# Folded column tiles: the accumulator's last big reader takes its scalar from PSUM, and the two extra columns are copied behind it

## The chip, the core and the metric

One NeuronCore of a Trainium2 chip runs the whole program. The metric is the device time of one execution in microseconds (us). TensorE (PE in the profile) multiplies, VectorE (DVE), ScalarE (ACT) and GpSimd (POOL) work on the results, SyncE (SP) issues loads. Matmul results land in PSUM, everything else lives in SBUF.

## What is computed

One inference step of a two-layer decoder with 256 prompt tokens and 32 sample tokens (8 sequences of 4), 288 token columns in all, model width 1024, in fp32. Per layer:

```python
proj = x @ w_in                       # q, k, v of 12 heads, and a gated unit
att  = dilated_window_attention(q, k, v)   # three head groups; sample tokens also see a cache
x = layer_norm(ALPHA * x + concat(att, sgu) @ w_mix_out, ln1_g, ln1_b)
qx = x @ w_xq;  x = layer_norm(ALPHA * x + cross_attention(qx, mem) @ w_xo, ln2_g, ln2_b)
h = square(relu(x @ w_up));  x = layer_norm(ALPHA * x + h @ w_down, ln3_g, ln3_b)
```

## The kernel before

The activations are kept transposed: 128 features on the partitions, 288 tokens along the free dimension. Each fp32 product is made of three matmuls of rounded parts (`L361` to `L363` in `mm3`): high weights by high activations (`wh`, `xH`), high by low (`wh`, `xL`), low by high (`wl`, `xH`). Weights stream in as 128 columns by 1024 rows; ScalarE rounds them to `wh` (`L343`) and VectorE forms the rest `wl` (`L344`). One output tile of 128 columns is 24 matmuls into one accumulator `acc`, of which there are three; so the fourth tile can start only when the first one's accumulator has been read out.

A layer norm would make TensorE wait: the next projection needs normalised activations. So the first tiles of the projection behind a norm are *folded*: they multiply the not yet normalised activations (`fH`, `fL`, already scaled by g), and the normalisation is done on the result. The operands carry two extra columns, minus g and b, so that a folded accumulator has 290 columns: 288 tokens, then the weights' column sums against minus g and b. `fold` turns such an accumulator into a tile `fy`: `L532` copies the two extra columns to a small SBUF tile `fw`, `L533` computes s * fw[0] + acc (s is the mean, one row of 288 on every partition), `L536` multiplies by q, the reciprocal deviation, on GpSimd for the first four folds of a norm and on VectorE after them. fw[1] goes on as the bias of whoever takes `fy`.

There are 32 folds in five stages: 8 tiles of `w_xq` in each layer, 6 of `w_up` in each layer, and 4 of `w_in` in layer 1. While they run, VectorE and GpSimd make the real normalised activations of the later tiles: `L611` or `L632` subtract the mean, `L615` or `L635` scale, `L625` or `L640` form `xL`. `w_in` of layer 1 has four folded tiles (queries 0 to 3) and then 18 tiles on `xH` and `xL`; its evacuation `evac_in` adds the bias (`L778`) and rotates queries and keys (`rope`: `L723`, `L724` on VectorE, `L725`, `L726` on GpSimd). Behind them come `L1041` and `L804` (transposes of `qT` and `kT`), `L984` (scores of the sample tokens, with `zq` from `L1015`) and, on GpSimd and VectorE, the products of cached keys with queries (`L1059`, `L1061`, `L1062`).

The order on each engine is not that of the code: a scheduler of the framework, which goes by a time model of its own, puts the instructions in order before the program is built. So a changed dependency can move other instructions too. On the chip every engine works its list strictly in order.

Of the kernel before, what the change touches and what calls it, by code (L numbers as in the profile page):

```python
# [12 lines left out]
ALU = mybir.AluOpType  # L13
# [7 lines left out]
TOK = SEQ + NS  # L21
# [207 lines left out]
def build(ctx, tc, I, O, worder, corder, recording):  # L229
    nc = tc.nc  # L230
    V, S, G, T = nc.vector, nc.scalar, nc.gpsimd, nc.tensor
# [8 lines left out]
    def etile(name="e", w=TOK):  # L240
        return sb.tile([128, w], F32, name=name, tag="e", bufs=8)
# [4 lines left out]
    def small(w, name="sm"):  # L246
        return sb.tile([128, w], F32, name=name, tag="small", bufs=12)
# [10 lines left out]
    def tr(name="tr"):  # L258
        return pp.tile([128, 512], F32, name=name, tag="tr", bufs=3)
# [197 lines left out]
    for n in range(KT):  # L457
        ps = tr()
# [40 lines left out]
    class LN:  # L499
# [28 lines left out]
        def fold(self, ps):  # L528

            w = small(2, "fw")  # L530
            e = etile("fy")
            V.tensor_copy(w, ps[:, TOK:TOK + 2])  # L532
            V.scalar_tensor_tensor(out=e, in0=self.s, scalar=w[:, 0:1], in1=ps[:, :TOK],  # L533
                                   op0=ALU.mult, op1=ALU.add)
            self.folds += 1
            (G if self.folds <= FOLD_POOL else V).tensor_mul(e, e, self.q)  # L536
            return e, w[:, 1:2]
# [969 lines left out]
```

## Time and profile before

| | us |
|---|---|
| median of 3 runs | 1071.11 |
| lowest, highest | 1068.39, 1072.94 |
| the profiled execution | 1073.84 |
| span of its records | 1072.1 |
| TensorE busy in the span | 1026.8 |
| VectorE busy in the span | 763.2 |

The span goes from the first to the last instruction; the profiled execution's own time is 1.7 us longer. Of all engines TensorE has the least idle time, 45 us.

### The profile page before, as it was taken

The page shows a single profiled execution, that of the slowest core. Times are in us where ns is not written, and L with a number is a line of the kernel's source. Part 1 is how long each engine was busy: PE and PEld are TensorE (multiplying, and loading weights), DVE is VectorE, ACT ScalarE, POOL GpSimd, SP SyncE. Part 2 cuts the span into 40 slices and gives each one's busy share as a digit, 9 for nine tenths or more (in the row PEclk, how much of TensorE's full clock was granted, in tenths as well). Part 3 has the DMA queues.
Part 4 walks back from the last instruction along what each step waited for, and adds up shares of the span by engine and source line. Part 5 has one row for each costly group of instructions (what it writes and reads, how often), then busy time and mean ns, then how long its engine had stood idle before and what let it go on. Part 6 is the DMA issues. An engine that isn't in the chain of part 4 may idle for free. (4 is left out here: it accounts for less than half of the span.)

```text
span 1072.1 us, 20130 instructions
## 1 busy us (share of the span) xinstructions
PE 1026.8 (96%) x8038; PEld 958.7 (89%) x8038; DVE 763.2 (71%) x1406; ACT 531.0 (50%) x1000; POOL 189.2 (18%) x151
## 2 busy tenths in 40 slices
PE   8999999999999999999988999999999999999995
PEld 7989589988799999999977985998888999999994
DVE  6698679855489756565996876897464996565656
ACT  4427546543458535353562364565353685354431
POOL 5592013000023000000448500220000410000000
PEclk8999999999999999999999999999999999999997
DMA  9999844777944555544455898447874465545431
GB/s 290 299 260 316 243 166 154 245 267 255 325 129 143 190 169 181 158 158 161 155 162 165 241 302 235 141 161 237 285 277 157 142 177 165 185 163 191 165 117 44
DMA packets 185533, 213.68 MB, mean 199 GB/s; under 512 B 5760, under 2 KB 175136, under 8 KB 185440
## 3 DMA queue, kind: packets, MB, share of 16 engines
q1 hardware_dynamic: 177216, 205.00, 60.1%
q10 hardware_dynamic: 8224, 7.41, 2.1%
q8 instruction: 63, 1.03, 0.4%
q14 instruction: 30, 0.25, 0.1%
HBM read 203.80 MB, written 8.59 MB: 198 GB/s over the span
## 5 line engine op out<-in xcount | busy, mean ns | idle before, releaser
L343 ACT ACTIVATE wh<-wraw 128x1024 fp32r<-128x1024 f32 (+1 forms) x237 | 249.3, 1054 | 285.6 <-PE acc L362 234.2
L344 DVE TENSOR_TENSOR wl<-wraw,wh 128x1024 fp32r<-128x1024 f32 (+1 forms) x237 | 308.4, 1304 | 100.1 <-ACT wh L343 99.5
L361 PE MATMUL acc<-xH,wh 128*128 128x288 f32 x728 | 219.0, 301 | 3.2 <-DVE fy L533 3.2
L363 PE MATMUL acc<-xH,wl 128*128 128x288 f32 x728 | 217.3, 299 | 2.7 <-DVE wl L344 2.7
L362 PE MATMUL acc<-xL,wh 128*128 128x288 f32 x728 | 218.5, 301 | 1.2 <-DVE xL L640 1.2
L361 PE MATMUL acc<-hH,wh 128*128 128x288 f32 x512 | 151.1, 295 | 0.0
L362 PE MATMUL acc<-hL,wh 128*128 128x288 f32 x512 | 151.1, 295 | 0.0
L363 PE MATMUL acc<-hH,wl 128*128 128x288 f32 x512 | 150.8, 295 | 0.0
L361 PEld LDWEIGHTS acc<-xH,wh 128*128 128x128 f32 x728 | 139.5, 192 | 4.4 <-issue 2.5
L363 PEld LDWEIGHTS acc<-xH,wl 128*128 128x128 f32 x728 | 138.9, 191 | 4.0 <-DVE wl L344 3.6
L362 PEld LDWEIGHTS acc<-xL,wh 128*128 128x128 f32 x728 | 139.1, 191 | 2.3 <-DVE xL L640 1.9
L551 POOL TENSOR_TENSOR s<-s,xres 128x288 f32<-128x288 f32 x15 | 20.2, 1349 | 444.8 <-DVE s L547 444.1
L361 PEld LDWEIGHTS acc<-hH,wh 128*128 128x128 f32 x512 | 96.4, 188 | 0.0
L362 PEld LDWEIGHTS acc<-hL,wh 128*128 128x128 f32 x512 | 96.4, 188 | 0.0
L363 PEld LDWEIGHTS acc<-hH,wl 128*128 128x128 f32 x512 | 96.2, 188 | 0.0
L361 PE MATMUL acc<-fH,wh 128*128 128x290 f32 x256 | 78.3, 306 | 1.8 <-DVE fy L533 1.8
L362 PE MATMUL acc<-fL,wh 128*128 128x290 f32 x256 | 76.9, 301 | 0.2 <-DVE fL L525 0.2
L363 PE MATMUL acc<-fH,wl 128*128 128x290 f32 x256 | 75.8, 299 | 0.5 <-DVE wl L344 0.5
L361 PEld LDWEIGHTS acc<-fH,wh 128*128 128x128 f32 x256 | 48.3, 189 | 2.6 <-PE acc L363 2.2
L362 PEld LDWEIGHTS acc<-fL,wh 128*128 128x128 f32 x256 | 48.5, 190 | 1.2 <-DVE fL L525 0.6
L363 PEld LDWEIGHTS acc<-fH,wl 128*128 128x128 f32 x256 | 48.1, 189 | 1.2 <-DVE wl L344 1.0
L1059 POOL TENSOR_TENSOR cu<-cu,qb 128x1024 f32<-128x1024 f32 x15 | 43.5, 2917 | 13.1 <-DMA qb<-qd 9.6
(326 smaller groups left out, 2182.2 us busy)
## 6 DMA issues: line engine op xcount, KB each, us to landing
cu<-cache_mem_kv SPq DMA_DIRECT2D x64, 512.0 KB, 7.4
wraw<-w_up SPq DMA_DIRECT2D x32, 1024.0 KB, 5.5
wraw<-w_down SPq DMA_DIRECT2D x32, 1024.0 KB, 4.8
wraw<-w_in SPq DMA_DIRECT2D x21, 1024.0 KB, 5.7
cu<-cache_kv_w SPq DMA_DIRECT2D x42, 512.0 KB, 8.5
wraw<-w_xkv SPq DMA_DIRECT2D x16, 1024.0 KB, 6.4
wraw<-w_mix_out SPq DMA_DIRECT2D x8, 1024.0 KB, 10.1
wraw<-w_xq SPq DMA_DIRECT2D x8, 1024.0 KB, 4.9
```

Source lines behind the costliest of these rows:

```text
L343: S.activation(h[:, r], raw[:, r], AF.Copy)
L344: gates[f"split{k}"] = behind(V.tensor_sub(lo[:, r], raw[:, r], h[:, r].bitcast(F32)), "dve")
L361: m = T.matmul(ps, wh[:, k], H[:, k], start=first, stop=False)
L362: T.matmul(ps, wh[:, k], L[:, k], start=False, stop=False)
L363: T.matmul(ps, wl[:, k], H[:, k], start=False, stop=last)
L551: eng.tensor_add(self.s, self.s, xres[:, n])
L1059: G.tensor_mul(cu, cu, qb[g])
```

## The change

`fold` issues its two VectorE operations the other way round, and the first of them reads its per-partition scalar from the accumulator itself, from column 288 in PSUM, where it read the copy in SBUF before. The copy of the two columns then only serves the bias. In the changed kernel the big operation is `L532` (to `L533`) and the copy is `L534`; all other lines keep their numbers.

```diff
             w = small(2, "fw")
             e = etile("fy")
+            V.scalar_tensor_tensor(out=e, in0=self.s, scalar=ps[:, TOK:TOK + 1], in1=ps[:, :TOK],
+                                   op0=ALU.mult, op1=ALU.add)
             V.tensor_copy(w, ps[:, TOK:TOK + 2])
-            V.scalar_tensor_tensor(out=e, in0=self.s, scalar=w[:, 0:1], in1=ps[:, :TOK],
-                                   op0=ALU.mult, op1=ALU.add)
             self.folds += 1
             (G if self.folds <= FOLD_POOL else V).tensor_mul(e, e, self.q)
             return e, w[:, 1:2]
```

The scheduler answers with another order in all five stages. First VectorE in `w_in` of layer 1, from the first scaling of the norm on; the first pair of lines that differ belongs to the second folded tile (rows with - are of before, with + of the change):

```order
 L635 SCALAR_TENSOR_TENSOR xres<-xres,lnp,q 128x288
-L532 COPY fw<-acc 128x2
+L532 SCALAR_TENSOR_TENSOR fy<-s,acc 128x288
+L534 COPY fw<-acc 128x2
 L635 SCALAR_TENSOR_TENSOR xres<-xres,lnp,q 128x288 x7
 L778 TENSOR_SCALAR fy<-fy,fw 128x288
 L344 TENSOR_TENSOR wl<-wraw,wh 128x1024
 L971 COPY kt<-tr 128x512
-L533 SCALAR_TENSOR_TENSOR fy<-s,fw,acc 128x288
-L640 SCALAR_TENSOR_TENSOR xL<-xres,lnp,xH 128x288 x5
-L532 COPY fw<-acc 128x2
+L640 SCALAR_TENSOR_TENSOR xL<-xres,lnp,xH 128x288
```

Before, the copy stood early and the big operation ten instructions later, just ahead of the `xL` tiles; now both stand at the copy's old place.

On TensorE in the same stage, the changed kernel, from the sixth k-step of the first tile that isn't folded (`acc_6354`; the tile after it is `acc_6389`, the third `acc_6430`):

```order
L361 MATMUL acc_6354<-xH_6122,wh_6244 128x288
L361 MATMUL acc_6389<-xH_6122,wh_6278 128x288
L362 MATMUL acc_6389<-xL_6123,wh_6278 128x288
L362 MATMUL acc_6354<-xL_6123,wh_6244 128x288
L363 MATMUL acc_6354<-xH_6122,wl_6245 128x288
L361 MATMUL acc_6354<-xH_6122,wh_6244 128x288
L363 MATMUL acc_6389<-xH_6122,wl_6279 128x288
```

Before, all 24 matmuls of `acc_6354` stood ahead of the first one of `acc_6389`; now the second tile begins between the last k-steps of the first.

On VectorE in `w_up` (the same in both layers), before, from the eight scalings of the norm to the second folded tile's big operation and the `wl` behind it:

```order
L615 SCALAR_TENSOR_TENSOR xres<-xres,lnp,q 128x288 x8
L532 COPY fw<-acc 128x2
L344 TENSOR_TENSOR wl<-wraw,wh 128x1024
L1438 TENSOR_TENSOR r<-r 128x288
L532 COPY fw<-acc 128x2
L533 SCALAR_TENSOR_TENSOR fy<-s,fw,acc 128x288
L344 TENSOR_TENSOR wl<-wraw,wh 128x1024
```

And the same place in the changed kernel:

```order
L615 SCALAR_TENSOR_TENSOR xres<-xres,lnp,q 128x288 x8
L344 TENSOR_TENSOR wl<-wraw,wh 128x1024
L1438 TENSOR_TENSOR r<-r 128x288
L532 SCALAR_TENSOR_TENSOR fy<-s,acc 128x288
L534 COPY fw<-acc 128x2
L344 TENSOR_TENSOR wl<-wraw,wh 128x1024
```

Here the big operation of the second tile stays where it was, behind `L344` and `L1438`; only two copies ahead of it are gone.

## Rows read from the trace of the kernel before

**Rows 1.** Page, part 1: busy us (share of the span) and instructions of each engine.

```profile
PE 1026.8 (96%) x8038; PEld 958.7 (89%) x8038; DVE 763.2 (71%) x1406; ACT 531.0 (50%) x1000; POOL 189.2 (18%) x151
```

**Rows 2.** Waits of PE: who waited, for whom, us in total, times, longest.

```profile
PE acc L361 <- DVE fy L533: 5.0, 4, 2.1
```

**Rows 3.** Stretches: length, busy (x instructions) of PE, PEld, DVE, ACT, POOL; PEclk, DMA.

```profile
164.00:205.00 41.00, 40.84 (x306) 39.63 (x306) 40.54 (x72) 26.77 (x50) 7.80 (x8) 1.00 0.61 202
528.00:562.00 34.00, 28.50 (x194) 26.17 (x192) 33.59 (x66) 20.42 (x40) 14.82 (x15) 0.95 0.51 159
552.00:558.00 6.00, 4.73 (x26) 4.76 (x27) 6.00 (x12) 0.17 (x1) 4.79 (x5) 0.72 0.46 159
562.00:600.00 38.00, 32.97 (x238) 30.17 (x238) 29.87 (x46) 12.40 (x24) 33.72 (x22) 0.91 0.57 180
586.00:594.00 8.00, 7.20 (x30) 5.96 (x31) 8.00 (x10) 0.84 (x2) 8.00 (x6) 0.57 0.65 214
```

**Rows 4.** Timeline of PE: start, us, instruction, [idle before, releaser].

```profile
335.24 0.37 PE L361 MATMUL acc<-fH,wh 128*128 128x290 f32 x1 [0.93 <-DVE fy L533]
...
545.59 0.37 PE L361 MATMUL acc<-xH,wh 128*128 128x288 f32 x1 [1.09 <-DVE fy L533]
...
546.90 0.40 PE L362 MATMUL acc<-xL,wh 128*128 128x288 f32 x1 [0.31 <-DVE xL L640]
...
550.68 0.40 PE L362 MATMUL acc<-xL,wh 128*128 128x288 f32 x1 [0.90 <-DVE xL L640]
...
553.27 0.58 PE L361 MATMUL acc<-xH,wh 128*128 128x288 f32 x1 [2.07 <-DVE fy L533]
...
556.21 0.30 PE L361 MATMUL acc<-xH,wh 128*128 128x288 f32 x1
...
557.82 0.29 PE L361 MATMUL acc<-xH,wh 128*128 128x288 f32 x1
...
564.78 0.28 PE L1041 MATMUL tr<-const,qT 128*32 128x128 f32 x1 [1.34 <-POOL qT L726]
...
586.04 0.40 PE L363 MATMUL acc<-xH,wl 128*128 128x288 f32 x1 [1.80 <-DVE wl L344]
```

**Rows 5.** Timeline of DVE in `w_in` of layer 1.

```profile
539.85 0.15 DVE L532 COPY fw<-acc 128x2 f32<-128x2 f32 x1
539.92 3.08 DVE L635 SCALAR_TENSOR_TENSOR xres<-xres,lnp,q 128x288 f32<-128x288 f32 x7
...
544.94 0.50 DVE L533 SCALAR_TENSOR_TENSOR fy<-s,fw,acc 128x288 f32<-128x288 f32 x1
545.36 2.77 DVE L640 SCALAR_TENSOR_TENSOR xL<-xres,lnp,xH 128x288 fp32r<-128x288 f32 x5
...
548.98 1.21 DVE L344 TENSOR_TENSOR wl<-wraw,wh 128x1024 fp32r<-128x1024 f32 x1
...
552.62 0.93 DVE L533 SCALAR_TENSOR_TENSOR fy<-s,fw,acc 128x288 f32<-128x288 f32 x2
```

**Rows 6.** Timeline of DVE in `w_up` of layer 0.

```profile
334.59 0.50 DVE L533 SCALAR_TENSOR_TENSOR fy<-s,fw,acc 128x288 f32<-128x288 f32 x1
```

**Rows 7.** Timeline of POOL in `w_in` of layer 1.

```profile
553.21 1.77 POOL L536 TENSOR_TENSOR fy<-fy,q 128x288 f32<-128x288 f32 x2 [6.67 <-DVE fy L533]
...
575.82 9.08 POOL L1059 TENSOR_TENSOR cu<-cu,qb 128x1024 f32<-128x1024 f32 x3 [2.13 <-issue]
584.86 3.53 POOL L725 TENSOR_TENSOR ro<-ro,const 128x288 f32<-128x288 f32 x2
```

**Rows 8.** Lines: instructions, min/median/max ns, first and last start, shape.

```profile
L532 DVE COPY fw<-acc x32: 143/149/160, 171.5 to 871.7; 128x2 f32<-128x2 f32 x32
L533 DVE SCALAR_TENSOR_TENSOR fy<-s,fw,acc x32: 498/502/515, 172.1 to 872.9; 128x288 f32<-128x288 f32 x32
L558 DVE TENSOR_TENSOR xres<-xres,acc x28: 434/442/455, 155.5 to 849.9; 128x288 f32<-128x288 f32 x28
L575 DVE TENSOR_TENSOR xres<-xres,c x15: 450/452/460, 151.7 to 834.0; 128x288 f32<-128x288 f32 x15
```

## The prediction

> **What bounds the kernel now.** The page's busy times come first: TensorE works 1026.8 us of a span of 1072.1 us [rows 1], VectorE, the engine that the change touches, 763.2 us. So only what shortens TensorE's 45 us of idle time, or raises its clock, can move the end. The second view is the list of TensorE's waits: it waited for `L533`, the operation that the change reorders, four times, 5.0 us in all [rows 2]. That is 0.47% of the time, and the most that the change can take away directly. The timeline gives the places: 0.93 us at 335.24 in `w_up` of layer 0, 1.09 us at 545.59 and 2.07 us at 553.27 in `w_in` of layer 1 [rows 4]; the remaining 0.9 us is the twin of the first, in `w_up` of layer 1. None is in `w_xq`, though it holds half of all folds. [...]
>
> **The price of the operation.** No row shows a scalar read from PSUM. From below it costs nothing more than the 502 ns of `L533`, and a gain is excluded, since the same 288 elements pass. From above, a separate read of such columns is a whole copy of 149 ns [rows 8]. The nearest row is a tensor from PSUM against one from SBUF in the same operation: 442 ns (`L558`) against 452 ns (`L575`) [rows 8], so PSUM is not dearer, and I take 0. The upper end is 0.15 us on each of 32 folds, 4.8 us of VectorE's time, of which 0.15 us each would lie ahead of a TensorE wait in `w_up` and some 0.5 us in `w_in`.
>
> [...]
>
> **w_xq, twice, and the rest.** TensorE is busy for 40.84 of 41 us there [rows 3], with no wait for `L533`, so nothing is to be had. The work that hides the fold is TensorE's own queue of matmuls and transposes. VectorE is just as full (40.54 of 41), so a dearer operation would show here first. The new order only moves transposes of cached keys into `w_xkv`, which TensorE must do anyway. I take 0, plus or minus 0.5 us.
>
> **w_up, twice.** TensorE waits at 335.24 for the big operation of the second fold, which started at 334.59 [rows 4, 6]. In the new order that operation keeps its place behind `L344` and `L1438`. Two copies ahead of it are gone, each 0.07 us of VectorE's time from start to start (539.85 to 539.92 [rows 5]), but the copy behind it now reads the accumulator last, 0.07 us plus a slightly later end. Gain 0.05 us each, 0.1 us in all. The 1.8 us in `w_up` stay.
>
> **w_in of layer 1.** The second fold's big operation moves from 544.94 to 539.85. What TensorE waits for at 545.59 is so free five us earlier. But the next thing that this tile needs is `xL`. The first `L640` stood at 545.36, right behind the operation that leaves. The same work as before stands ahead of it: 0.07 for the copy, 0.42 for the big operation (544.94 to 545.36), and all that lay between 539.92 and 544.94, 5.02 us [rows 5]. 539.85 + 0.07 + 0.42 + 5.02 = 545.36: the same time to the hundredth. So the wait of 1.09 us is handed from `L533` to `L640`, and nothing is won.
>
> The wait at 553.27 is another matter. The third fold's operation was the first of the two that start at 552.62, behind the `xL` tiles, two `L344` and a bias. Now it comes after five `L640` and one bias: five at 0.42 us are 2.1 (the five took 2.77 us, with one held up [rows 5]), the bias I take at 0.4 us, as the plain operations of its size [rows 8]. 545.36 + 2.5 = 547.9, and with the operation and its copy 548.4. So the accumulator that `acc_6389` needs is free at 548.4 instead of 553.1, and the scheduler lets TensorE start that tile between the last steps of `acc_6354`. What is late next is its `wl`, an `L344` that started at 548.98 and now starts behind the sixth `L640`, at 548.8; with its 1.21 us [rows 5] TensorE waits for it until 550.0. From there 27 matmuls of the two tiles are left, at 0.134 us each (12 of them between 556.21 and 557.82 [rows 4]): 3.6 us, so `acc_6430` starts at 553.6, where it started at 557.82. These 4.2 us contain the wait of 2.07 us, the lost clock of 1.7 us, and part of the waits for `xL` of 0.31 and 0.90 us (546.90 and 550.68 [rows 4]).
>
> Not all of that is kept. VectorE does two `L640` behind that `L344` and then the fourth fold, which ends at 550.0 + 0.8 + 0.5 = 551.3; then four rope operations and the `wl` of `acc_6430`, some 1.8 and 1.2 us, so until 554.3: 0.4 us go back. Then TensorE runs into GpSimd: the queries must pass through `L536`, `L725`, `L726`. GpSimd began its last two `L536` at 553.21, after 6.67 us of idle time [rows 7]; now the fourth fold is there at 551.3, so the queries can come 1.9 us earlier, not 4.2. The fourth tile also needs VectorE to have read `acc_6354`, behind four more rope operations and a `wl`. Between 0 and 1.9 us for the transposes `L1041` (564.78 before [rows 4]) I take 0.6; 18 matmuls of the fourth tile now stand ahead of them, 2.4 us that are done by then. About 3.0 us kept; bounds 1.5 (half of the 18 matmuls held up too) and 4.3.
>
> **Sum.** 0.1 + 3.0 + 0 = 3.1 us of the profiled execution's 1073.84 us, 0.3%. The median of the runs shown is 1071.11; the same gain makes it 1068.0 us. A measurement of this kernel tells 0.5%, 5.4 us, from no change, so this forecast falls under "the same".
>
> **Rivals.**
> *The second stall goes too.* The `wl` that TensorE waits for at 586.04 stands on VectorE behind reductions of what GpSimd multiplies (`L1062` behind `L1059`). In the new order one or two of these reductions come behind it. If it is in time, 1.8 us of wait and 3.4 us of clock come on top: 1068.0 - 5.2 = 1062.8 us. For it speaks the new order; against it, that TensorE arrives 3 us earlier and the `L1059` start when the query load has landed, which hardly moves, so the slack is under 1 us by my count.
> *Nothing is kept.* GpSimd is busy 33.72 of the 38 us from 562 to 600 [rows 3]. If queries and keys come when they came before, TensorE waits for them instead: 1071 us. Against it: GpSimd was idle for 6.67 us just before and can use an earlier fold [rows 7].
> *Slower.* In the new order the rotation `L726` of the second head group's first key tile stands on GpSimd behind the three `L1059` (9.08 us [rows 7]), and two `L725` and another `L726` come after it; before, two `L725` of 3.53 us stood behind them. If the query load lands half a microsecond earlier, the second key tile is there at 575.3 + 9.1 + 3.5 + about 2 for two `L726` = 589.9. TensorE stood at 584.24 before it waited until 586.04; 3 us earlier, plus one tile of 24 x 0.134 us and about 1 us of transposes, it would need that key tile at 585.5. A wait of 4.4 us, with 3.4 to 6.8 us of clock behind it (as after 586.04, or in proportion to a wait twice as long): 1068.0 + 4.4 + 5.1 = 1077.5 us. [...] Against it: the loss at 586 would then be gone, and the other engines catch up while TensorE stands.
>
> **How the numbers follow.** Chances: the forecast 0.50, the second stall gone 0.25, nothing kept 0.11, slower 0.14. The forecast's own range is 1066.5 to 1069.8, from its bounds of 4.3 + 0.1 + 0.5 us and 1.5 + 0.1 - 0.5 us. With the second case's 1062.8 and a little below it, and above with nothing kept, the dearer scalar (0.8 us on the path) and the nearer part of the slower case, 8 in 10 lie between 1061.5 and 1075. Faster by over 0.5% (below 1065.8): the second case and a little of the first, 0.28. Slower (above 1076.5): most of the slower case, 0.11. The same: 0.61.
>
> **What the profile after would show.** The big operation at about 502 ns; the waits for the fold in `w_in` gone, with waits for `xL` and then for `wl` and `qT` in their place; the `w_up` waits of 0.9 us unchanged; `acc_6430` near 553.6 and full clock from 552 to 558. I am wrong if the operation is 0.1 us longer or more, if the first wait in `w_in` vanishes, or if the stretch from 562 to 600 changes by more than the stage before it.

## The result, and the profile after

The changed kernel takes 1083.64 us (median of 6 runs, 1081.56 to 1085.25); the kernel before took 1073.06 us in the same session (6 runs). The ratio is 1.0105, with a 95% interval of 1.0084 to 1.0126: slower by 1.05%, some 11 us. Forecast were 1068.0 us and "the same"; the time lies above the range of 1061.5 to 1075.0. The profiled execution took 1081.97 us with a span of 1080.2 us, 8.1 us more than the one before.

First the changed operation itself. Durations of the two instructions of a fold, ns min/median/max:

```profile
L532 DVE SCALAR_TENSOR_TENSOR fy<-s,acc x32: 503/509/521, 171.7 to 880.3; 128x288 f32<-128x288 f32 x32
L534 DVE COPY fw<-acc x32: 145/150/155, 172.1 to 880.7; 128x2 f32<-128x2 f32 x32
```

The multiply-add with its scalar in PSUM takes 509 ns where the one with the scalar in SBUF took 502 [rows 8], the copy 150 where it took 149.

Now the stretches, with the same columns as in [rows 3], first of the changed kernel:

```profile
543.00:558.00 15.00, 11.83 (x75) 11.14 (x74) 15.00 (x30) 10.19 (x21) 7.63 (x6) 0.89 0.48 151
544.00:600.00 56.00, 45.90 (x323) 42.61 (x322) 47.83 (x81) 23.21 (x44) 42.71 (x30) 0.91 0.51 159
546.00:550.00 4.00, 3.69 (x16) 3.46 (x17) 4.00 (x10) 3.12 (x7) 1.29 (x1) 0.64 0.33 110
552.00:558.00 6.00, 4.75 (x36) 4.51 (x35) 6.00 (x13) 3.35 (x8) 5.41 (x5) 1.00 0.47 162
562.00:600.00 38.00, 32.93 (x239) 30.76 (x238) 29.83 (x43) 12.57 (x23) 32.54 (x22) 0.91 0.54 169
580.00:588.00 8.00, 5.96 (x25) 5.96 (x26) 8.00 (x7) 0.51 (x1) 8.00 (x4) 0.58 0.60 196
600.00:640.00 40.00, 34.10 (x240) 32.11 (x238) 34.37 (x62) 18.38 (x40) 6.67 (x2) 0.91 0.92 277
612.00:626.00 14.00, 9.94 (x55) 9.18 (x54) 12.95 (x15) 2.85 (x6) 6.67 (x2) 0.76 0.65 210
```

and of the kernel before:

```profile
543.00:558.00 15.00, 10.62 (x62) 9.50 (x62) 15.00 (x30) 7.67 (x14) 5.74 (x6) 0.89 0.56 172
544.00:600.00 56.00, 46.17 (x323) 41.77 (x321) 47.87 (x83) 22.35 (x43) 43.46 (x31) 0.91 0.57 181
600.00:640.00 40.00, 38.53 (x282) 36.51 (x281) 31.28 (x69) 23.02 (x51) 5.78 (x2) 0.96 0.98 303
612.00:626.00 14.00, 14.00 (x111) 13.92 (x109) 13.58 (x28) 9.26 (x20) 2.68 (x2) 1.00 1.09 366
```

Up to 600 us the two come out alike: from 544 to 600 us TensorE works off 323 matmuls in either kernel, at a mean granted clock of 0.91. Between 600 and 640 us TensorE is busy 34.10 us instead of 38.53, and from 612 to 626 us it gets through 55 instructions instead of 111, at a granted clock of 0.76. Counting the 24 matmuls of each tile, the changed kernel began the last matmul of its 13th unfolded tile of `w_in` 2.2 us ahead of the kernel before (612.7 against 614.9), and that of the 14th 7.0 us behind (626.0 against 619.0). The 2.2 us are no lead over all work, since TensorE's other matmuls stand at other places in the new list. It stays about 8 us behind to the end.

What TensorE waits for there. Waits of PE in the changed kernel (us in total, times, longest):

```profile
PE acc L363 <- DVE wl L344: 6.7, 7, 3.2
PE s L1074 <- DVE zs L1068: 3.8, 1, 3.8
...
PE acc L362 <- DVE xL L640: 1.9, 1, 1.9
PE acc L361 <- DVE ro L724: 1.9, 1, 1.9
...
PE acc L361 <- DVE fw L534: 1.7, 2, 0.9
```

In the kernel before, the waits for `wl` were:

```profile
PE acc L363 <- DVE wl L344: 3.2, 6, 1.8
```

The wait for the fold is 1.7 us where it was 5.0 [rows 2]; the 3.3 us are gone, but the waits for `wl` grew by 3.5 us. New are two waits of 1.9 us, for the first `xL` and for a rotation (`L724`) that frees an accumulator, and one wait of 3.8 us for `zs`, the tile that VectorE makes from the sample tokens' products with the first group of cached keys (`L1068`). Timeline of VectorE around it (start, us, instruction, idle before), in the changed kernel:

```profile
577.47 1.23 DVE L1061 TENSOR_TENSOR cu<-cu,qb 128x1024 f32<-128x1024 f32 x1 [4.96 <-DMA qb<-qd]
...
578.82 3.17 DVE L344 TENSOR_TENSOR wl<-wraw,wh 128x1024 fp32r<-128x1024 f32 x1
...
608.02 1.22 DVE L344 TENSOR_TENSOR wl<-wraw,wh 128x1024 fp32r<-128x1024 f32 x1
613.05 1.23 DVE L1061 TENSOR_TENSOR cu<-cu,qb 128x1024 f32<-128x1024 f32 x1 [3.81 <-DMA qb<-qd]
614.19 3.36 DVE L1068 TENSOR_TENSOR zs<-st,const 128x1024 f32<-128x1024 f32 x1
617.48 3.37 DVE L344 TENSOR_TENSOR wl<-wraw,wh 128x1024 fp32r<-128x1024 f32 x1
...
630.06 0.68 DVE L1068 TENSOR_TENSOR zs<-st,const 128x512 f32<-128x512 f32 x1
```

and in the kernel before:

```profile
575.72 1.22 DVE L1061 TENSOR_TENSOR cu<-cu,qb 128x1024 f32<-128x1024 f32 x1 [2.68 <-DMA qb<-qd]
...
605.89 1.21 DVE L1068 TENSOR_TENSOR zs<-st,const 128x1024 f32<-128x1024 f32 x1
607.03 1.21 DVE L344 TENSOR_TENSOR wl<-wraw,wh 128x1024 fp32r<-128x1024 f32 x1
608.86 1.23 DVE L1061 TENSOR_TENSOR cu<-cu,qb 128x1024 f32<-128x1024 f32 x1 [0.62 <-DMA qb<-qd]
...
622.78 0.69 DVE L1068 TENSOR_TENSOR zs<-st,const 128x512 f32<-128x512 f32 x1
```

The scheduler has put the second query group's product `L1061` ahead of `L1068`. `L1061` needs the second query load (`qb`), which has not landed; VectorE stands for 3.81 us, and `L1068` behind it, which needs nothing of that load, stands too. GpSimd begins its own two products at the same moment, and beside them `L1068` takes 3.36 us instead of 1.21. GpSimd in the changed kernel (the profile names a load of cached keys as the last thing that it waited for):

```profile
613.09 3.38 POOL L1059 TENSOR_TENSOR cu<-cu,qb 128x1024 f32<-128x1024 f32 x1 [13.70 <-DMA cu<-cache_kv_w]
616.44 3.33 POOL L1059 TENSOR_TENSOR cu<-cu,qb 128x1024 f32<-128x1024 f32 x1
```

The first query load does the same on a smaller scale: VectorE stands 4.96 us for it at 577.47, where it stood 2.68 us before, and TensorE's wait of 3.25 us at 582.04 is for the `wl` of 578.82, which stands behind that product. On TensorE, in order, the waits of the changed kernel of 0.7 us and more in `w_in` up to the one for `zs`:

```profile
546.26 0.40 PE L362 MATMUL acc<-xL,wh 128*128 128x288 f32 x1 [1.86 <-DVE xL L640]
...
556.10 0.40 PE L363 MATMUL acc<-xH,wl 128*128 128x288 f32 x1 [1.25 <-DVE wl L344]
...
561.48 0.40 PE L361 MATMUL acc<-xH,wh 128*128 128x288 f32 x1 [1.86 <-DVE ro L724]
...
565.85 0.28 PE L1041 MATMUL tr<-const,qT 128*32 128x128 f32 x1 [0.70 <-POOL qT L726]
...
582.04 0.61 PE L363 MATMUL acc<-xH,wl 128*128 128x288 f32 x1 [3.25 <-DVE wl L344]
...
599.45 0.41 PE L1001 MATMUL sc<-kT,zn 128*128 128x32 f32 x2 [1.13 <-POOL kT L726]
...
617.61 2.56 PE L1074 MATMUL s<-const,zs 128*128 128x16 f32 x16 [3.77 <-DVE zs L1068]
```

The load itself also comes later. SP's queue in the changed kernel, and below it in the kernel before (`L755` is the first load of the stage's spatial bias; it serves as the stage's zero mark below):

```profile
539.79 1.80 SPq L755 DMA_DIRECT2D misc<-b_spatial  x3
...
570.55 0.65 SPq L1048 DMA_DIRECT2D qb<-qd  x1
...
600.50 0.37 SPq L148 DMA_DIRECT2D wraw<-w_in  x1
603.35 0.62 SPq L1048 DMA_DIRECT2D qb<-qd  x1
```

```profile
540.57 2.48 SPq L755 DMA_DIRECT2D misc<-b_spatial  x4
...
568.04 0.64 SPq L1048 DMA_DIRECT2D qb<-qd  x1
...
600.74 0.62 SPq L1048 DMA_DIRECT2D qb<-qd  x1
...
602.50 0.54 SPq L148 DMA_DIRECT2D wraw<-w_in  x1
```

Both query loads are requested some 2.5 us later, and the second now stands behind the last `w_in` load, which it stood ahead of; VectorE has its data at 613.05 instead of 608.86.

### The profile page after: what moved, and what is told of

The parts are those of the page before. It is cut to its first block, busy times and chain, and to the rows that moved or that the text cites. A ratio compares the mean times of both kernels' runs of the same rounds, so it can differ in the third digit from the quotient of the medians.

```text
span 1080.2 us, 20135 instructions
## 1 busy us (share of the span) xinstructions
PE 1028.7 (95%) x8038; PEld 961.3 (89%) x8038; DVE 769.9 (71%) x1406; ACT 532.4 (49%) x1000; POOL 195.4 (18%) x151
## 5 line engine op out<-in xcount | busy, mean ns | idle before, releaser
L344 DVE TENSOR_TENSOR wl<-wraw,wh 128x1024 fp32r<-128x1024 f32 (+1 forms) x237 | 305.9, 1293 | 104.8 <-ACT wh L343 104.4
L363 PE MATMUL acc<-xH,wl 128*128 128x288 f32 x728 | 219.5, 302 | 5.0 <-DVE wl L344 5.0
```

The source lines that it names most:

```text
L344: gates[f"split{k}"] = behind(V.tensor_sub(lo[:, r], raw[:, r], h[:, r].bitcast(F32)), "dve")
L363: T.matmul(ps, wl[:, k], H[:, k], start=False, stop=last)
```

## The experiments

Theory 1: the change as such costs nothing, the loss is in the lists that the scheduler wrote in answer to it. Theory 2: the multiply-add with a PSUM scalar, or when it releases the accumulator, costs the time. Theory 3: `w_in` is reached earlier, and so the query loads meet other loads. Medians of the kernel before were 1070.0 to 1073.1 us from session to session, so each run is given by its ratio.

**The operation or the lists.** `e5_old_order_psum` keeps the instruction lists of the kernel before and exchanges one operand of the scheduled instruction:

```diff
-            V.scalar_tensor_tensor(out=e, in0=self.s, scalar=w[:, 0:1], in1=ps[:, :TOK],
+            m = V.scalar_tensor_tensor(out=e, in0=self.s, scalar=w[:, 0:1], in1=ps[:, :TOK],
...
+            if not recording:
+                SCALARS.append((m, None))
...
+                    ops[1] = nc.vector.lower_ap(ops[2].bass_ap.tensor[:, TOK:TOK + 1])
```

> The kernel before, with its instruction lists kept as they are on every engine: after the scheduling, the scalar of the 32 folds' multiply-add (L533) is read from column 288 of the accumulator in PSUM and no longer from the copied column. Only the operand differs. Theory 1 (the loss comes from the new order of VectorE's list, in which the second query group's product L1061 stands ahead of L1068): about 1073 us, within 0.3% of before, and L1068 starts near 605.9 us as before. Theory 2 (the multiply-add with a PSUM scalar, or its release of the accumulator, costs the time itself): about 1084 us. Theory 3 (the earlier arrival at w_in puts the query's DMAs beside other loads): about 1073 us, since nothing arrives earlier.

Measured: 1070.99 us, ratio 0.9998 (0.9981 to 1.0014).

`e3_copy_first` leaves the copy first, but has the program read the scalar from PSUM, so that the scheduler sees two operations that don't depend on each other:

```diff
             V.tensor_copy(w, ps[:, TOK:TOK + 2])
-            V.scalar_tensor_tensor(out=e, in0=self.s, scalar=w[:, 0:1], in1=ps[:, :TOK],
+            V.scalar_tensor_tensor(out=e, in0=self.s, scalar=ps[:, TOK:TOK + 1], in1=ps[:, :TOK],
```

> The scalar comes from PSUM in the program itself, but the copy stays ahead of the multiply-add, so the accumulator is released as late as before; the two no longer depend on each other, and the scheduler's list on VectorE puts L1061 ahead of L1068, almost as in the changed kernel. Theory 1: about 1083 us (1080 to 1086), with a TensorE wait of 3 to 4 us at L1074 for zs and the clock at half behind it. Theory 2: about 1084 us if it is the operand, 1073 us if it is the place of the copy. Theory 3: about 1073 us, since the copy ahead holds the release where it was.

Measured: 1083.11 us, 1.0118 (1.0077 to 1.0159), with a wait of 2.9 us for `zs`. The two kernels have the same operand; only the lists differ. When the program is built with the dependency on the copy put back beside the PSUM scalar, as one that synchronises, the scheduler writes the old lists again, row for row; a dependency that only orders the two leaves it with the lists of `e3` (these programs were built, not run). So it is the lost dependency that it answers to.

**Which folds.** `e1_not_win` and `e2_only_win` choose the form by stage (`self.j < 2` is `w_xq` and `w_up`, `self.j == 2` the four folds of `w_in`):

```diff
+            if self.j < 2:
+                V.scalar_tensor_tensor(out=e, in0=self.s, scalar=ps[:, TOK:TOK + 1], in1=ps[:, :TOK],
...
+            else:
+                V.tensor_copy(w, ps[:, TOK:TOK + 2])
```

> The new form in the 28 folds of w_xq and w_up, the old form in the four of w_in. The list on VectorE has L1068 (here five lines further down) ahead of L1061 again, as before. Theory 1: 1068 to 1076 us, and no TensorE wait over 1 us for zs. Theory 2: 28 of 32 parts of the loss of 10.6 us, 9.3 us, so about 1082 us. Theory 3: about 1073 us, since w_in is not reached earlier.

Measured: 1071.52 us, 0.9997 (0.9978 to 1.0015).

> The new form in the four folds of w_in alone, the old form in the other 28; the lists are the scheduler's, and SP's and GpSimd's come out as in the changed kernel, VectorE's with L1061 ahead of L1068. Theory 1 (the lists around w_in of layer 1): 1081 to 1085 us, all of the loss. If the loss came with the number of new folds: 4 of 32 parts, 1073 to 1074 us.

Measured: 1083.91 us, 1.0103 (1.0057 to 1.0149). Four folds of 32 bring the whole loss.

**The change in the old lists.** Here the program is scheduled twice without being run, in the old form and in the new, and the lists that result are forced on the kernel by dependencies that only order; `OLD` names the engines that get the old list, the others get the new one (`REST` is "new" in all these runs):

```python
    lists = [(old if e in OLD else new if REST == "new" else {}).get(e) for e in ("PE", "DVE", "Activation", "Pool", "SP")]
...
        for names in lists or ():
            names = [n for n in names if n in traced]
            for first, then in zip(names, names[1:]):
                tc.add_manual_dep(traced[then], first, dep, reason="list")
```

`e11_old_lists` has all five old:

> All 32 folds in the new form (scalar from PSUM, copy directly behind), but every engine's instruction list is the one of the kernel before, forced by order-only dependencies; each copy alone is moved, to behind its multiply-add. This is the change as such without the new lists. Theory 1 (all of the loss is in the lists): 1071 us, within 0.3% of before. The forecast's own sum for it was a gain of a few us from the earlier release: 1068 us. Theory 2 (operand or release cost the time): 1082 us.

Measured: 1072.24 us, 1.0000 (0.9976 to 1.0023). Its multiply-adds take as long as the changed kernel's:

```profile
L533 DVE SCALAR_TENSOR_TENSOR fy<-s,acc x32: 500/506/520, 170.4 to 871.9; 128x288 f32<-128x288 f32 x32
```

Theory 1 holds and theory 2 falls. Theory 3 can't be the whole: `e14` below loses 5 us though nothing arrives earlier in it. No run forces all five new lists on the kernel in the same way, so what the forcing itself does to the mixed lists below was not measured; with the old lists it costs nothing.

**The displaced product.** `e4_zs_gate` orders `L1061` of the second group behind `L1068` in the changed kernel:

```diff
-                        behind(V.tensor_mul(cu, cu, qb[g]), lag)
+                        behind(behind(V.tensor_mul(cu, cu, qb[g]), lag), f"zs{l}" if g == 2 else "")
...
+                    gates[f"zs{l}"] = zm
```

> The changed kernel with one order-only dependency more: the second query group's products on VectorE (L1061) stand behind the first group's L1068. The other rows of VectorE's list stay, save for some ten of them. Theory 1: the TensorE wait of 3.77 us at L1074 goes, and with it about 3.4 us of the half clock from 618 to 626 us: 1083.6 - 7.2 = 1076 us (1073 to 1079). Theory 2: about 1083 us. Theory 3: about 1083 us, since arrival and loads stay, with the second query's load landing near 613 us.

Measured: 1079.69 us, 1.0082 (1.0056 to 1.0108): by the ratios 2.5 us better than the changed kernel, not 7, and the intervals overlap. The wait for this `zs` is gone, but VectorE still stands in front of `L1061`, and the next thing queued behind it, the maxima `L910`, is now what TensorE waits for. VectorE and TensorE in this kernel:

```profile
612.80 1.23 DVE L1061 TENSOR_TENSOR cu<-cu,qb 128x1024 f32<-128x1024 f32 x1 [3.17 <-DMA qb<-qd]
```

```profile
619.11 1.11 PE L804 MATMUL tr<-const,vt 128*128 128x128 f32 x4 [2.97 <-DVE m L910]
```

`e7_early_old` does the reverse: in the kernel before, that product is written out ahead of `L1068`.

```diff
+                if l and g == 1:
+                    for j in range(2):
+                        ahead[2, j] = cs.request(("g2", l, j, 0), 1)
+                        done.append((2, j))
+                    G.tensor_mul(ahead[2, 0], ahead[2, 0], qb[2])
+                    gates["early"] = behind(V.tensor_mul(ahead[2, 1], ahead[2, 1], qb[2]), lag)
...
+                    behind(zm, "early")
```

> The kernel before, folds untouched; only the first product of the second query group on VectorE (L1061, here L1075) is written out ahead of L1068 and of the weight split behind it, as the changed kernel has it in its list. Theory 1 (VectorE's queue stands still behind L1061 until the second query's load has landed, and L1074 waits for zs behind it): slower without the new folds. In the kernel before that load lands at 608.9 us and L1068 runs from 605.9 to 607.0; here L1068 would end between 611 and 613.5 us where L1074 is due at 610.0: 1 to 3.5 us of wait and as much again by the lower clock behind it, so 1073 to 1079 us, 1076 taken. Theories 2 and 3 (operand or release; arrival and loads): 1072 us.

Measured: 1076.39 us, 1.0041 (1.0015 to 1.0067). That is 4.4 us; the displaced product is a part of the 11 us, not all of them. The ten runs spread from 1070.5 to 1081.2 us, and the one with the profile is the fastest.

**Taking away its wait.** `e8_late_product` adds `if l and g == 2 and j == 1: yield 0, 4000` ahead of the product, so that it stands behind everything that waited; `e10_late_product_old` is the same in the kernel before; `e9_early_query` sets `QUERY_2 = 3` instead of 4, so that the second query is loaded one product earlier.

> The changed kernel with the second group's first product on VectorE put later in layer 1: the product, which waits for the second query's load, stands behind L1068, the next weight split, the maxima L910 and the probabilities L929. Theory 1: neither zs nor the maxima are late any more, no TensorE wait over 1 us for them: 1083.6 less 3.8 of wait, 3.4 of half clock and up to 3 of waits that stood behind it, 1073 to 1077 us; what is left over 1071.8 is another place. Theories 2 and 3: 1083 us.

Measured: 1086.78 us, 1.0141 (1.0101 to 1.0181).

> The kernel before with the same later place of the second group's first product. Theory 1: there VectorE stood only 0.62 us for the load, so little is to be had: 1069 to 1073 us. If e8 gains more than this by much, its gain is the mended wait and not the later place in itself.

Measured: 1078.01 us, 1.0056 (1.0037 to 1.0075).

> The changed kernel with the second query's load requested one product earlier (after the fourth instead of the fifth of the first group), in both layers; on SP's queue it then stands ahead of two of the w_in loads, where the changed kernel has it behind the last one. VectorE's list still has L1061 ahead of L1068. Theory 1: the load lands before VectorE comes to L1061, so the wait for zs goes though the order stays: 1073 to 1078 us. If the order alone were at fault, whatever the load does: 1083 us. Theory 2: 1083 us.

Measured: 1083.24 us, 1.0109 (1.0070 to 1.0149). In `e8` TensorE waits 0.7 us for `zs`, in `e9` not at all, and nothing is won. In `e8` the next link is late:

```profile
PE o L1130 <- DMA cu<-cache_kv_w: 6.7, 3, 5.3
```

(`L1130` is `L1128` here, the weighted sum of cached values.) So taking away the wait for `zs` mended none of these kernels. What it is worth by itself they don't show, since their edits rewrite the lists too: on VectorE some 44 rows stand elsewhere in `e8`, 47 in `e10` and 39 in `e9`, where `e4` moves 7 and `e7` only 2. What all these kernels share is that the sample tokens' chain is late: query load, products, `zs`, scores, softmax, values. A fourth theory: the time follows how late that chain is, wherever TensorE happens to wait for it.

**One engine's list at a time.** New lists for one engine among old ones:

> New form of the folds; VectorE has the list of the changed kernel (with L1061 ahead of L1068), all other engines have the lists of the kernel before. Theory A (the loss sits in VectorE's list): 1079 to 1084 us. Theory B (it sits in TensorE's list, which has the first query's transposes L1041 some tiles later): 1073 to 1076 us, no more than the 4 to 5 us that the one displaced product was worth. Theory C (it sits in SP's list, which has the second query's load behind the last w_in load): as B.

> New form of the folds; TensorE has the list of the changed kernel, all others those of the kernel before. Theory A: 1070 to 1073 us. Theory B: 1077 to 1084 us, with the first query's load requested some 2 to 3 us later in the stage. Theory C: 1070 to 1073 us.

> New form of the folds; SP has the list of the changed kernel (the last w_in load ahead of the second query's load), all others those of the kernel before. Theories A and B: 1070 to 1073 us. Theory C: 1077 to 1084 us, with the second query's load landing 4 us later in the stage.

Measured: 1087.88 us, 1.0143 (1.0125 to 1.0161) with VectorE's new list; 1080.98 us, 1.0087 (1.0071 to 1.0104) with TensorE's; 1078.04 us, 1.0048 (1.0029 to 1.0067) with SP's. None of A, B and C holds: each list loses, and the three losses add up to 30 us where all new lists together lose 11. SP's new list differs from the old one only in two `w_in` loads that stand earlier, one ahead of a load of cached keys, the last one ahead of the second query load and two loads of cached keys, and it costs 5 us: the second query load is late, and VectorE, whose list is the old one, stands longer at `L1061` than in the changed kernel (line numbers are five higher here). VectorE and TensorE in `e14`:

```profile
610.01 1.23 DVE L1066 TENSOR_TENSOR cu<-cu,qb 128x1024 f32<-128x1024 f32 x1 [5.18 <-DMA qb<-qd]
```

```profile
615.33 1.11 PE L809 MATMUL tr<-const,vt 128*128 128x128 f32 x4 [2.66 <-DVE m L915]
```

And one old list among new ones:

> The changed kernel, lists kept on all engines but SP, which gets the list of the kernel before (the second query's load again ahead of the last w_in load). Theory 4 (the loss is how late the second query group's scores come, whichever list delays them; VectorE's zs of that group came 82.2 us after the stage's b_spatial loads in the kernel before and 90.3 in the changed one, and the runs so far lost about 1.3 us for each us): the load lands some 4 us sooner, zs at about 86.5, 1077 to 1079 us. Theory A (VectorE's list alone decides): 1083 us. Theory C (SP's list decides): 1072 to 1074 us.

> The changed kernel, lists kept on all engines but VectorE, which gets the list of the kernel before, with each copy behind its multiply-add. Theory A: 1072 to 1074 us. Theory 4: the second query's load still lands late, since TensorE's and SP's lists are the new ones, so zs at 87 to 91 and 1078 to 1084 us.

> The changed kernel, lists kept on all engines but TensorE, which gets the list of the kernel before, with the first query's transposes earlier. Theory B (TensorE's list decides): 1072 to 1074 us. Theory 4: SP's list still has the second load late and VectorE's still puts L1061 ahead, so zs at 88 to 92 and 1079 to 1086 us.

Measured: 1080.15 us, 1.0087 (1.0062 to 1.0113) with SP's old list; 1092.41 us, 1.0177 (1.0129 to 1.0225) with VectorE's; 1090.42 us, 1.0163 (1.0106 to 1.0220) with TensorE's. Putting back the list of one engine doesn't mend the kernel, and with VectorE's or TensorE's it makes it worse: a list of one set among those of the other loses. TensorE in `e17`, where the old list comes to `zs` early and VectorE's new one delivers it late:

```profile
622.76 3.60 PE L1079 MATMUL s<-const,zs 128*128 128x16 f32 x16 [6.73 <-DVE zs L1073]
```

**The late chain, measured.** The fourth theory can be read off each profile: when does VectorE begin the second group's `zs` (the `L1068` of 512 elements), counted from the `L755` above? Before it is 622.78 - 540.57 = 82.2 us, after the change 630.06 - 539.79 = 90.3 us.

| kernel | second zs, us | ratio to before |
|---|---|---|
| before | 82.2 | 1 |
| e1, e5, e11 | 81.9, 81.6, 82.3 | 0.9997, 0.9998, 1.0000 |
| e7, e14 | 85.4, 86.7 | 1.0041, 1.0048 |
| e9 | 86.1 | 1.0109 |
| e4, e15, e10 | 88.8, 89.0, 89.2 | 1.0082, 1.0087, 1.0056 |
| after, e13 | 90.3, 90.9 | 1.0105, 1.0087 |
| e3, e12, e2 | 91.5, 91.9, 92.3 | 1.0118, 1.0143, 1.0103 |
| e16, e8, e17 | 93.5, 94.2, 98.1 | 1.0177, 1.0141, 1.0163 |

Without `e9`, a straight line through these 17 kernels has a slope of 1.26 us of time (ratio times 1072 us) per us of lateness, with a correlation of 0.96; with it the slope is 1.21 and the correlation 0.92. With each profiled execution's own span in place of the ratio the 17 give 0.91. It is one profile for each kernel, and from this `zs` to the end of the span all of them take 447 to 457 us (before 449.3, after 450.2): the loss lies between the mark and this `zs`, and whatever holds the engines up there would make the same line. So this is a strong sign, not a proof.

`e9` speaks against it. Its edit also changes layer 0, and it comes to the mark at 543.0 us, later than any other (535.9 to 541.7). But counted from the mark to the end it still takes 539.0 us, where the changed kernel takes 540.4 and the kernel before 531.5: its second `zs` came 4.2 us sooner than the changed kernel's and won 1.4 us.

`e15`, `e16` and `e17` were forecast by this theory and came out 1, 8 and 4 us above their ranges, in part because the forecast of the lateness was off (86.5, 87 to 91 and 88 to 92 us against 89.0, 93.5 and 98.1); `e16` lies 4.6 us above the line even at its measured lateness.

No kernel of these is faster than the kernel before.

## Why the prediction was wrong

Point by point, by its own steps:

- *The price of the operation*, taken as 0 with an upper end of 0.15 us: right. It is 7 ns (509 against 502), and `e5` and `e11` show that all 32 together cost nothing that can be measured (0.9998 and 1.0000). The tensor operand lies in PSUM in both forms, so for a tensor source this says nothing.
- *w_xq* at 0: right as far as `e1` tells, 0.9997 with 28 new folds in `w_xq` and `w_up`.
- *w_up* at 0.1 us, with the waits staying: right, 1.7 us in two waits of up to 0.9.
- *w_in, the first wait is handed to `L640`*: right: 1.86 us at 546.26 for `xL`, where 1.09 and 0.31 us stood [rows 4].
- *w_in, the third fold, then a wait for `wl`*: right in the main. The third tile (`acc_6430`) begins at 554.4 us by the count of matmuls, forecast 553.6, before 557.82. But no wait for `wl` until 550.0 is there. The stretch from 552 to 558 us, forecast at full clock, has 1.00 instead of 0.72 [rows 3], yet the lost clock that the sum counts as won, 6 us x 0.28 = 1.7 us, only moved: behind the wait of 1.86 us for `xL` it is 0.64 from 546 to 550 us, and from 543 to 558 us it is 0.89 in both kernels.
- *The sizing that failed*: "Not all of that is kept", priced at 0.4 us for the third tile's `wl` and 0.6 us won at the transposes. TensorE waited 1.25 us for that `wl` (556.10) and then 1.86 us for the accumulator of the fourth tile (561.48), a wait that the prediction names and gives no price of its own. These 3.1 us take back nearly all of the 3.4 us won at the third tile. The transposes `L1041` did not come 0.6 us earlier: the second ran at 565.85, 1.1 us later, and the query load behind them was requested 2.5 us later.
- *The step that failed*: "About 3.0 us kept", carried through the sum to the end of the kernel. None of it is kept: by 600 us TensorE has done the same 323 matmuls since 544 us in both kernels. And the new order was worked out up to the fourth fold, while the 60 us of lists behind it were taken to stay. They did not: there `L1061` moved ahead of `L1068` on VectorE, the second `qb` load behind a `w_in` load on SP, and `L984` and `L1041` on TensorE to other tiles. From 612 to 626 us the wait of 3.77 us for `zs` and 3.4 us of clock behind it make up 7.2 of the 8.1 us by which the profiled execution is longer. The term for the lists behind the fourth fold was put at nothing without a reason. In the old lists (`e11`) the change leaves the time as it is; the 3.0 us were worked out for the new ones.
- *The range*: its own bounds, 4.3 + 0.1 + 0.5 and 1.5 + 0.1 - 0.5 us, give 1066.2 to 1070.0 us, not 1066.5 to 1069.8. The measured time is far outside either.
- *The rivals*. "The second stall goes too" is wrong: it came at 582.04, 3.25 us long instead of 1.80, at a clock of 0.58 around it. "Nothing is kept", 1071 us, is what the profile shows up to 600 us, though TensorE waited more for VectorE than for queries and keys; the loss then comes on top. "Slower", 1077.5 us, had the right shape (a wait of 4.4 us in the second half of the stage, and clock behind it) and the wrong place: it was the keys behind GpSimd's products, where it was `zs` behind a product on VectorE that waits for a load. That its size comes near is luck. Its chance was 0.14, too little for a change that rewrites every list. The 3.4 us of clock in two of the rivals are 8 us x 0.43, by the stretch from 586 to 594 us [rows 3]; that the lost clock grows with the wait, as 3.4 to 6.8 us assume, was the author's estimate and is not what the profile after shows: behind the wait of 3.25 us it is 8 us x 0.42 = 3.4 us, behind 3.77 us 3.4 us, and behind the wait of 1.86 us at 561.48 the clock is 1.00 from 562 to 570 us.
- *What would show me wrong* was "if the stretch from 562 to 600 changes by more than the stage before it". It did not (32.93 us of TensorE against 32.97); the loss lies between 612 and 626 us, beyond the last place that I had thought of.

What stays open: which rows of the lists, beyond the displaced product (2.5 us back in `e4`, 4.4 us in `e7`) and SP's two moved loads (5 us alone), make up the rest; the parts do not add. And that the lateness of the sample tokens' chain is the cause of the time, not only its companion, is not shown: kernels that make it late in lists near the old ones are slower (`e7`, `e14`, and `e10`, which moves more rows), but the one that makes it earlier in lists near the new ones, `e9`, wins next to nothing.

## What to carry to other kernels

When a scheduler orders the engines, the price of an edit is that of the new lists, not of the operation: compare the lists of all engines to the end of the stage, and look for an instruction that waits for a load and has moved ahead of one that doesn't. Measure the edit in the old lists as well (here 1.0000 against 1.0105), so that a good edit isn't dropped, or a neutral one credited, for what the scheduler made of it. A wait that the profile names may only be where a late chain surfaces: if taking it away wins nothing (`e8`, `e9`), time the chain against a mark as well.

## What the runs showed of the hardware

A 128x1024 operation of two tensors on VectorE took 1.21 us with GpSimd idle (`L1068` and `L344` at 605.89 and 607.03 in the kernel before) and 3.36 us beside GpSimd's products of the same size (614.19 and 617.48 in the changed kernel). The records end in turn: `L1061` at 614.28, GpSimd's first product at 616.47, `L1068` at 617.55, GpSimd's second at 619.77, `L344` at 620.85, that is, one of GpSimd 2.2 us after one of VectorE, and one of VectorE 1.1 us after one of GpSimd. `L1061`, which starts with the first product, keeps its 1.23 us, and the 24 reductions of one tensor (`L1062`) took 1.20 to 1.22 us, 1.21 us for the one at 581.91, beside GpSimd's products. Reductions in the changed kernel:

```profile
L1062 DVE TENSOR_REDUCE st<-cu x24: 1203/1206/1220, 58.4 to 627.7; 128x16 f32<-128x1024 f32 x24
```

The reorder caused this slowing as well: standing right behind `L1061`, `L1068` starts when the load lands, and so does GpSimd. After the 3.77 us wait at 617.61 TensorE's granted clock was 0.57 from 618 to 626 us (0.50 from 619 to 625 us), where the kernel before had 1.00:

```profile
618.00:626.00 8.00, 7.70 (x39) 7.22 (x39) 8.00 (x13) 1.24 (x3) 1.77 (x1) 0.57 0.38 109
```

That is another 8 x 0.43 = 3.4 us, nearly as much as the wait itself.

In the trace of the kernel before, the operations of VectorE (1382), GpSimd (147) and ScalarE (963, its loads aside) start in the order of their lists, and so do the 300 loads and stores that SP issues; on TensorE the records of four pairs of `L902` and `L906` stand the other way round.
